# The last tile's store cut into three transfers, and other hand-over semaphores, in a scores kernel

## The chip, the cores and the metric

The kernel runs on one core of one Trainium2 chip. The metric is the device time of one execution in microseconds (us), the median of several runs. The core has a matrix engine (TensorE, PE in the profile), three engines that work on elements (VectorE or DVE, ScalarE or ACT, GpSimd or POOL), an engine that only issues transfers and handles semaphores (SyncE, SP), and 16 DMA engines that move data between the chip's main memory and the on-chip buffers. TensorE's results arrive in a small accumulation memory (PSUM), from which ACT and DVE copy them into the large on-chip memory (SBUF); stores to main memory start from there.

## The reference

```
batch, heads, seq, dim = 8, 8, 512, 64        # q and k: float32
scale = 1.0 / sqrt(dim)
out = einsum('bhqd,bhkd->bhqk', q, k) * scale # float32, 8 x 8 x 512 x 512
```

For each of the 64 pairs of batch and head, the product of q and the transposed k, scaled. The inputs are 16.8 MB, the output is 67.1 MB.

## The kernel before, in words

**Units and tiles.** The inputs are handled in four units of two batches (`UNITS`). A unit's k and q are loaded by one transfer each of 2 MB (`load`, L80). The output is produced in 16 tiles of 4 MB (`CHUNKS * UNITS`). A tile covers four heads of one batch: 128 rows (partitions), each with two runs of 16 KB that are contiguous in main memory (`out_r[g]`, L46). A tile is held in one of three SBUF buffers `bigs`, which serve as load buffers at the start and as store buffers afterwards (`store_buffer`, L77: buffers 0, 2, 1 in turn).

**Preparing the operands.** POOL casts the loaded float32 to bf16 (`cast`, L126, into `xb`, in places straight into `xs`). For each unit there are four chunks that must be transposed. From the second unit on, POOL copies a chunk from `xb` into the staging buffer `xs` (`fill`, L121), PE transposes it into the PSUM tile `tp` (`turn`, L164), and ACT and DVE each move a half of it into the operand buffers `kT` (keys) and `qz` (queries) (`move`, L214). One chunk is handled within each of the first 12 tiles, between its third and fourth pair of matmuls.

**Computing a tile.** PE runs a loop over the 16 tiles (L200). A tile has eight steps p, each with two matmuls that fill one of three PSUM buffers `pss[p % 3]` (`scores`, L182). ACT evicts the even steps and DVE the odd ones, with the scaling, into the store buffer (`evacuator`, L231). The order on every engine is written out by hand, and the engines hand over by semaphores.

**Semaphores.** `next` lets PE begin a tile. `free0a` to `free2b` say that a PSUM buffer has been evicted; six names alternate, as the lists `before` and `after` (L176) have it. PE waits for one of them, and the first matmul behind the wait counts it down again when it completes (L190). `ready` says that a chunk lies in `xs`, `turn` that PE has transposed it, `moved` that ACT and DVE have put it away, `cast` and `room` that load buffers have been read.

**SP.** SP issues everything that moves between main memory and SBUF. For each tile it waits until both evictors have ended their last step (`out`, two counts a tile), issues the store of 4 MB as one transfer, then waits until the store two tiles earlier has landed (`landed`, L98; for the first two tiles, until POOL has read the load buffer, `room`), and only then raises `next`. So a tile starts when the store buffer it writes is free, and SP's issue of the store before it stands in that chain. Each transfer counts a semaphore up by 16 when it has landed.

**POOL at the end.** Behind the casts, POOL copies ten chunks into `xs` (L159 to L161), each as soon as PE has transposed the chunk before it.

Of the kernel before, what the change touches and what calls it, by code (L numbers as in the profile page):

```python
# [5 lines left out]
def kernel(  # L6
# [5 lines left out]
    nc = tc.nc  # L12
    B, H, S, D = q.shape
    scale = 1.0 / (D ** 0.5)
    P = 128
    UNITS = B // 2
# [4 lines left out]
    RO = 8  # L21
# [6 lines left out]
    CHUNKS = 4  # L28
    SLOTS = 12
    PAIRS = RO  # L30
# [4 lines left out]


    names = ["ready", "room", "moved", "zeroed", "ident", "turn", "pe_act", "pe_dve",
             "next", "free0a", "free0b", "free1a", "free1b", "free2a", "free2b",
             "out", "cast"]
    sem = {name: nc.alloc_semaphore(name) for name in names}  # L40
    load_sems = [nc.alloc_semaphore(f"load{n}") for n in range(2 * UNITS)]
    store_sems = [nc.alloc_semaphore(f"store{n}") for n in range(3)]

    q_r = q.rearrange("(v b) g (m j) d -> v (b g m) (j d)", b=2, j=R)
    k_r = k.rearrange("(v b) g (m j) d -> v (b g m) (j d)", b=2, j=R)
    out_r = out.rearrange("(v b) (t x h) (u i) k -> (v b t) (h u) x (i k)", b=2, x=2, h=2, i=RO)  # L46
# [5 lines left out]
    qz = nc.alloc_sbuf_tensor("qz", [P, 2 * N, RO, P], bf16)[:]  # L52
    identity = nc.alloc_sbuf_tensor("identity", [P, P], f32)[:]
    tp = nc.alloc_psum_tensor("tp", [P, W, P], f32)[:]
    pss = [nc.alloc_psum_tensor(f"ps{n}", [P, 2, S], f32)[:] for n in range(3)]

    def words(ap):
        return ap.bitcast(f32)
# [7 lines left out]
    xsw = words(xs.rearrange("p w s d e -> p w (s d e)"))  # L66
    keys = kT.rearrange("p n m s j -> p n (m s j)")

    pe = nc.tensor
# [7 lines left out]
    def store_buffer(g):  # L77
        return bigs[(0, 2, 1)[g % 3]]

    def load(v, x):  # L80
        nc.sync.dma_start(out=xf(v)[:, x],
                          in_=(k_r, q_r)[x][v].rearrange("p (s c) -> p s c", s=2)
                          ).then_inc(load_sems[2 * v + x], 16)
# [6 lines left out]
    tc.compile()  # L90


    nc.sync.wait_ge(sem["room"], 1)
    nc.sync.sem_inc(sem["next"], 1)
    for x in range(2):
        nc.sync.wait_ge(sem["cast"], x + 1)
        load(UNITS - 1, x)
    def landed(g):  # L98
        nc.sync.wait_ge(store_sems[g % 3], 16 * (g // 3 + 1))

    for g in range(CHUNKS * UNITS):
        nc.sync.wait_ge(sem["out"], 2 * g + 2)
        nc.sync.dma_start(out=out_r[g], in_=store_buffer(g).rearrange("p x i k -> p x (i k)")  # L103
                          ).then_inc(store_sems[g % 3], 16)
        if g < CHUNKS * UNITS - 1:
            if g >= 2:
                landed(g - 2)
            else:
                nc.sync.wait_ge(sem["room"], g + 2)
            nc.sync.sem_inc(sem["next"], 1)  # L110
    for n in range(3):
        nc.sync.wait_ge(store_sems[n], 16 * len(range(n, 4 * UNITS, 3)))


    nc.gpsimd.memset(identity, 0.0).then_inc(sem["ident"], 1)
# [2 lines left out]
                            fill=1.0, base=0, pattern=[[-1, P]], channel_multiplier=1  # L118
                            ).then_inc(sem["ident"], 1)

    def fill(copy, c):  # L121
        w0 = c % SLOTS * W
        copy(out=xs.rearrange("p w s d e -> p (w s d e)"),  # L123
             in_=xb[:, w0:w0 + W].rearrange("p w s d e -> p (w s d e)")).then_inc(sem["ready"], 1)

    def cast(v, x, s, j0, j1, dst):  # L126
        src = xf(v)[:, x, s]
        if x == 0:
            src = src.rearrange("p (j e d) -> p j e d", e=2, d=D)[:, j0:j1]
            dst = dst[:, :, s].rearrange("p j d e -> p j e d")  # L130
        else:
            src = src.rearrange("p (j e i d) -> p j e i d", e=2, i=RO, d=D)
            dst = dst[:, :, s].rearrange("p (i j) d e -> p j e i d", i=RO)
        return nc.gpsimd.tensor_copy(out=dst, in_=src)  # L134

    for v in range(UNITS):
        for x in range(2):
# [4 lines left out]
            if v == 1 and x == 0:  # L142
# [3 lines left out]
                last = cast(v, x, 1, 0, W, xs)  # L146
                last.then_inc(sem["ready"], 1)
            else:
                for s in range(2):
                    last = cast(v, x, s, 0, JP, xb[:, w0:w0 + JP])  # L150
# [5 lines left out]
                nc.gpsimd.drain().then_inc(sem["cast"], 1)  # L156
            elif v == 1 and x == 1:
                last.then_inc(sem["cast"], 1)
    for c in range(CHUNKS + 2, CHUNKS * UNITS):  # L159
        nc.gpsimd.wait_ge(sem["turn"], c)  # L160
        fill(nc.gpsimd.tensor_copy, c)  # L161


    def turn(src, dst):  # L164
        for w in range(W):
            ins = pe.transpose(out=dst[:, w], identity=identity, in_=src[:, w])  # L166
            if w == 0 and dst is tp and src is xsw:
                ins.then_inc(sem["ready"], -1)
        ins.then_inc(sem["turn"], 1)

    def take(name, count=1):
        pe.wait_ge(sem[name], count).then_inc(sem[name], -count)  # L172

    before = ["next", None, "free2a", "free0a", "free1a", "free2b", "free0b", "free1b"]  # L176
    after = ["free0a", "free1a", "free2b", "free0b", "free1b", "free2a", "out", "out"]

    def weights(n2, p, w):
        return qz[:, bass.ds(n2 + p // 4, 1), p % 4 * 2 + w].rearrange("p n c -> p (n c)")  # L180

    def scores(n2, p):  # L182
        for w in range(2):
            if w == 0 and before[p]:
                pe.wait_ge(sem[before[p]], 1)
            ins = pe.matmul(out=pss[p % 3][:, w, :], lhsT=weights(n2, p, w),  # L186
                            rhs=keys[:, bass.ds(n2 + p // 4, 1)].rearrange("p n c -> p (n c)"),
                            start=True, stop=True)
            if w == 0 and before[p]:
                ins.then_inc(sem[before[p]], -1)  # L190
        ins.then_inc(sem["pe_dve" if p % 2 else "pe_act"], 1)

    pe.wait_ge(sem["ident"], 2)
# [1 line left out]
    for c in range(CHUNKS):  # L195
        take("ready")
        turn(xw[:, c * W:(c + 1) * W], first[c])
    take("moved", 4 * CHUNKS)
    pe.sem_inc(sem["free2a"], 1)
    with pe.Fori(0, CHUNKS * UNITS) as g:  # L200
        n2 = g % (2 * TILES) * 2
        for p in range(3):
            scores(n2, p)
        with pe.If(g < CHUNKS * (UNITS - 1)):
            pe.wait_ge(sem["ready"], 1)
            turn(xsw, tp)
        for p in range(3, PAIRS):
            scores(n2, p)
        with pe.If(g < CHUNKS * (UNITS - 1)):
            take("moved", CHUNKS)  # L210
# [3 lines left out]
    def move(copy, c, s, tile_):  # L214
        v, t = divmod(c, CHUNKS)
        n0 = v % 2 * N
        h0 = t % 2 * W
        if t < 2:
            src = tile_[half(s)].rearrange("d j (n h m) -> d h n m j", n=N, h=2)
        else:  # L220
            src = tile_[half(s)].rearrange("d (i jj) (n h m) -> d h i n m jj", jj=JJ, n=N, h=2)
            h0 = t % 2 * IW
        for h in range(2):
            if t < 2:
                dst = kw[half(h), n0:n0 + N, :, s, h0:h0 + W]
            else:
                dst = qw[half(h), n0:n0 + N, h0:h0 + IW, h * U // 2:(h + 1) * U // 2].rearrange(
                    "d n i (m s jj) -> d s i n m jj", s=2, jj=JJ)[:, s]
            copy(out=dst, in_=src[:, h]).then_inc(sem["moved"], 1)  # L229

    def evacuator(engine, copy, scaled, parity, done):  # L231
        if parity:
            for v in range(2):
                engine.memset(qz[:, v * N:(v + 1) * N], 0.0).then_inc(sem["zeroed"], 1)  # L234
        for c in range(CHUNKS):
            engine.wait_ge(sem["turn"], c + 1)
            if c == 2:
                engine.wait_ge(sem["zeroed"], 2)
            move(copy, c, parity, first[c])
        count = 0  # L240
        for g in range(CHUNKS * UNITS):
            o = store_buffer(g)
            for p in range(parity, PAIRS, 2):
                x, i = p // 4, p % 4 * 2
                count += 1
                engine.wait_ge(done, count)
                scaled(o[:, x, i:i + 2, :], pss[p % 3]).then_inc(sem[after[p]], 1)
                c = g + CHUNKS
                if p in (1, 2) and c < CHUNKS * UNITS:
                    engine.wait_ge(sem["turn"], c + 1)  # L250
                    move(copy, c, parity, tp)
            if g == 0 and not parity:
                fill(copy, CHUNKS + 1)

    evacuator(nc.scalar, nc.scalar.copy,
              lambda o, ps: nc.scalar.mul(out=o, in_=ps, mul=scale),  # L256
              0, sem["pe_act"])
    evacuator(nc.vector, nc.vector.tensor_copy,
              lambda o, ps: nc.vector.tensor_scalar(out=o, in0=ps, scalar1=scale, scalar2=None,  # L259
                                                    op0=mult),  # L260
              1, sem["pe_dve"])


# [28 lines left out]
```

## Time and profile before

| | |
|---|---|
| Runs | 202.41, 202.66 and 202.81 us; median 202.66 |
| Profiled execution | 202.81 us, of which the span from the first to the last instruction is 201.5 (201.46) us |
| Moved | 16.78 MB read, 67.11 MB written; 416 GB/s over the span |
| Stores | 16, each 4 MB, issued at 32.1 to 180.3 us; 14.9 to 22.2 us from issue to landing, 17.9 in the median |
| Loads | 8, each 2 MB |
| Matmuls of the scores (L186) | 256, mean 469 ns |
| Evictions | DVE 64, mean 1223 ns; ACT 64, mean 1024 ns |
| POOL casts (L134) | 16, mean 2322 ns; copies into `xs` (L123) 10, mean 1896 ns |

How to read it: the profile gives, for each engine, the time in which it executed instructions; a slice view cuts the span, or a window of it, into 40 equal parts and gives the busy share in tenths, for DMA the mean over the 16 DMA engines, with the bytes moved below it. A window view gives the busy time of each engine in a stretch, the granted clock of TensorE, the DMA share and the rate. The chain of waits follows the work that ended last back from step to step. `SPq` is SP's instruction sequence, where issues and semaphore operations lie; L followed by a number is a line of the kernel. "Issue to landing" is the time from a transfer's issue until all engines that carry it have reported.

### The profile page before, as it was taken

Reading aid. Unit: us, or ns where it says so; the run is one execution under the profiler, and the core shown is the slowest. Engines: PE = TensorE matmul, PEld = TensorE weight load, DVE = VectorE, ACT = ScalarE, POOL = GpSimd, SP = SyncE. Lnnn points to the kernel's source line nnn. Section 1 sums busy time; section 2 is a strip of 40 time slices with the busy share of each in tenths; the row PEclk is TensorE's granted clock in tenths of the full one; section 3 lists DMA queues with packets and bytes.
Section 4 is the critical chain, followed back from the end, with each engine's and each line's share of the span. In section 5 each row is a group of like instructions: output and inputs, shape, how many; then the busy total and the mean of one; then the engine's idle time right before and its main releaser. Section 6 shows DMA issues by size and latency. Waiting matters only on the chain.

```text
span 201.5 us, 1491 instructions
## 1 busy us (share of the span) xinstructions
PE 102.4 (51%) x384; PEld 51.4 (25%) x384; DVE 106.1 (53%) x98; ACT 87.4 (43%) x98; POOL 58.4 (29%) x34
## 2 busy tenths in 40 slices
PE   0027481275756575753939394657546575750000
PEld 0026240132424243431506051333112121210000
DVE  0666673074747576768384856957562727260000
ACT  0205665073746464655555464756543434440000
POOL 0399999999303030302121130300000000000000
PEclk9999979588888888799696969978885858575555
DMA  5999999999999999999999999999999999999993
GB/s 185 429 429 439 433 426 423 439 403 436 426 426 446 426 423 431 434 429 420 449 426 423 439 436 423 426 442 429 420 436 436 423 433 436 429 416 426 439 429 137
DMA packets 5506, 83.90 MB, mean 416 GB/s; under 512 B 384, under 2 KB 384, under 8 KB 384
## 3 DMA queue, kind: packets, MB, share of 16 engines
q1 hardware_dynamic: 5504, 83.89, 97.9%
q14 instruction: 2, 0.02, 0.0%
HBM read 16.78 MB, written 67.11 MB: 416 GB/s over the span
## 4 chain that ended last, share of the span: by engine, by line
PE 28%; DVE 21%; DMA 15%; POOL 14%; POOLq 5%; issue 4%; SPq 2%; ACT 1%
PE ps L186 20%; DVE big L259 15%; POOL xb L134 13%; DMA out_dram<-big 11%; PE tp L166 7%; POOLq L154 5%; DVE qz L229 4%; DMA big<-in_k_dram 4%; DVE kT L229 2%; SPq L103 2%; POOL xs L134 1%; POOLq L156 1%; ACT big L256 1%; SPq L110 0%; SPq L90 0%
## 5 line engine op out<-in xcount | busy, mean ns | idle before, releaser
L186 PE MATMUL ps<-kT,qz 128*128 x256 | 81.7, 469 | 61.4 <-SPq L110 42.0
L259 DVE TENSOR_SCALAR big<-ps 128x1024 f32<-128x1024 f32 x64 | 77.0, 1223 | 52.0 <-PE ps L186 50.6
L256 ACT ACTIVATE big<-ps 128x1024 f32<-128x1024 f32 x64 | 65.3, 1024 | 70.2 <-PE ps L186 69.9
L186 PEld LDWEIGHTS ps<-kT,qz 128*128 x256 | 28.4, 111 | 106.9 <-issue 96.9
L134 POOL CAST xb<-big 128x2048 bf16<-128x2048 f32 (+1 forms) x16 | 36.2, 2322 | 3.6 <-DMA big<-in_k_dram 3.1
L123 POOL COPY xs<-xb 128x2048 bf16<-128x2048 bf16 x10 | 19.0, 1896 | 62.0 <-PE tp L166 61.9
L166 PE MATMUL tp<-identity,xs 128*128 128x128 f32 x96 | 19.8, 376 | 0.0
L166 PEld LDWEIGHTS tp<-identity,xs 128*128 128x128 f32 x96 | 18.2, 206 | 4.7 <-issue 4.1
L229 DVE COPY kT<-tp 64x512 f32<-64x512 f32 x14 | 9.7, 694 | 9.1 <-PE tp L166 8.9
L229 ACT COPY kT<-tp 64x512 f32<-64x512 f32 x14 | 8.1, 579 | 13.1 <-PE tp L166 12.9
L229 DVE COPY qz<-tp 64x512 f32<-64x512 f32 x12 | 8.3, 695 | 4.9 <-PE tp L166 4.6
L234 DVE MEMSET qz<- 128x4096 uint32 x2 | 6.9, 3472 | 6.8 <-PEq L90 6.0
L166 PE MATMUL tp<-identity,xb 128*128 128x128 f32 x8 | 1.9, 424 | 13.9 <-PEq L172 13.9
L229 ACT COPY qz<-tp 64x512 f32<-64x512 f32 x12 | 7.5, 622 | 2.1 <-PE tp L166 2.0
L166 PEld LDWEIGHTS tp<-identity,xb 128*128 128x128 f32 x8 | 1.6, 224 | 13.8 <-issue 13.8
L166 PE MATMUL ps<-identity,xb 128*128 128x128 f32 x24 | 3.9, 323 | 1.2 <-PEq L172 1.2
L166 PEld LDWEIGHTS ps<-identity,xb 128*128 128x128 f32 x24 | 3.5, 171 | 1.6 <-issue 1.6
L229 ACT ACT_TABLE_LOAD x1 | 1.3, 1283 | 5.0 <-PEq L90 5.0
L229 DVE COPY qz<-ps 64x512 f32<-64x512 f32 x4 | 2.8, 694 | 1.0 <-PE ps L166 0.9
L229 ACT COPY qz<-ps 64x512 f32<-64x512 f32 x4 | 2.5, 629 | 1.2 <-PE ps L166 1.1
L134 POOL CAST xs<-big 128x1024 bf16<-128x1024 f32 x2 | 2.7, 1337 | 0.2 <-DMA big<-in_k_dram 0.2
L123 ACT COPY xs<-xb 128x2048 bf16<-128x2048 bf16 x1 | 1.9, 1890 | 0.0
(8 smaller groups left out, 3.5 us busy)
## 6 DMA issues: line engine op xcount, KB each, us to landing
out_dram<-big SPq DMA_DIRECT2D x16, 4096.0 KB, 17.9
big<-in_k_dram SPq DMA_DIRECT2D x4, 2048.0 KB, 15.5
big<-in_q_dram SPq DMA_DIRECT2D x4, 2048.0 KB, 17.8
```

The lines of the kernel that those rows point to most:

```text
L103: nc.sync.dma_start(out=out_r[g], in_=store_buffer(g).rearrange("p x i k -> p x (i k)")).then_inc(store_sems[g % 3], 16)
L123: copy(out=xs.rearrange("p w s d e -> p (w s d e)"), in_=xb[:, w0:w0 + W].rearrange("p w s d e -> p (w s d e)")).then_inc(sem["ready"], 1)
L134: return nc.gpsimd.tensor_copy(out=dst, in_=src)
L154: nc.gpsimd.drain().then_inc(sem["room"], 1)
L156: nc.gpsimd.drain().then_inc(sem["cast"], 1)
L166: ins = pe.transpose(out=dst[:, w], identity=identity, in_=src[:, w])
L186: ins = pe.matmul(out=pss[p % 3][:, w, :], lhsT=weights(n2, p, w), rhs=keys[:, bass.ds(n2 + p // 4, 1)].rearrange("p n c -> p (n c)"), sta ...
L229: copy(out=dst, in_=src[:, h]).then_inc(sem["moved"], 1)
L234: engine.memset(qz[:, v * N:(v + 1) * N], 0.0).then_inc(sem["zeroed"], 1)
L256: lambda o, ps: nc.scalar.mul(out=o, in_=ps, mul=scale),
L259: lambda o, ps: nc.vector.tensor_scalar(out=o, in0=ps, scalar1=scale, scalar2=None, op0=mult),
```

## The change

Three things change.

**The last store.** The first 15 tiles are stored as before. The last tile's store is issued as three transfers: the first 12 KB of every 16 KB run, of all 128 rows; the last 4 KB of each run of rows 0 to 119; the last 4 KB of each run of rows 120 to 127. Each has its own semaphore, and SP waits for all three at the end.

**Who raises what.** SP raises `next` as soon as both evictors have finished a tile, before it issues the store, and no longer waits for an earlier store to land. POOL does that waiting: behind each of its copies into `xs` it waits for the store two tiles back and raises `room`. PE takes `next` before the first matmul of a tile and `room` before the second.

**How PE waits.** The six `free` names become three, and `out` becomes one name for each evictor. PE's wait and the count-down are one instruction ahead of the matmul (`take`), where before the matmul carried the count-down.

```diff
-    nc.sync.wait_ge(sem["room"], 1)
-    nc.sync.sem_inc(sem["next"], 1)
     for x in range(2):
         nc.sync.wait_ge(sem["cast"], x + 1)
         load(UNITS - 1, x)
-    def landed(g):
-        nc.sync.wait_ge(store_sems[g % 3], 16 * (g // 3 + 1))
-
+    edge = 3 * RO * S // 4
+    parts = [(slice(0, P), slice(0, edge)), (slice(0, P - 8), slice(edge, RO * S)),
+             (slice(P - 8, P), slice(edge, RO * S))]
+    last = CHUNKS * UNITS - 1
     for g in range(CHUNKS * UNITS):
-        nc.sync.wait_ge(sem["out"], 2 * g + 2)
-        nc.sync.dma_start(out=out_r[g], in_=store_buffer(g).rearrange("p x i k -> p x (i k)")
-                          ).then_inc(store_sems[g % 3], 16)
-        if g < CHUNKS * UNITS - 1:
-            if g >= 2:
-                landed(g - 2)
-            else:
-                nc.sync.wait_ge(sem["room"], g + 2)
-            nc.sync.sem_inc(sem["next"], 1)
+        nc.sync.wait_ge(sem["out_act"], g + 1)
+        nc.sync.wait_ge(sem["out_dve"], g + 1).then_inc(sem["next"], 1)
+        src = store_buffer(g).rearrange("p x i k -> p x (i k)")
+        if g < last:
+            nc.sync.dma_start(out=out_r[g], in_=src).then_inc(store_sems[g % 3], 16)
+        else:
+            for n, (rows, cols) in enumerate(parts):
+                nc.sync.dma_start(out=out_r[g][rows, :, cols], in_=src[rows, :, cols]
+                                  ).then_inc(part_sems[n], 16)
...
-    for c in range(CHUNKS + 2, CHUNKS * UNITS):
-        nc.gpsimd.wait_ge(sem["turn"], c)
-        fill(nc.gpsimd.tensor_copy, c)
+    for g in range(2, CHUNKS * UNITS - 1):
+        if g + CHUNKS < CHUNKS * UNITS:
+            nc.gpsimd.wait_ge(sem["turn"], g + CHUNKS)
+            fill(nc.gpsimd.tensor_copy, g + CHUNKS)
+        nc.gpsimd.wait_ge(store_sems[(g - 2) % 3], 16 * ((g - 2) // 3 + 1)
+                          ).then_inc(sem["room"], 1)
...
     def scores(n2, p):
+        x, i = p // 4, p % 4 * 2
+        if p != 1:
+            take(f"free{p % 3}" if p else "next")
+        ps = pss[p % 3]
         for w in range(2):
-            if w == 0 and before[p]:
-                pe.wait_ge(sem[before[p]], 1)
-            ins = pe.matmul(out=pss[p % 3][:, w, :], lhsT=weights(n2, p, w),
-                            rhs=keys[:, bass.ds(n2 + p // 4, 1)].rearrange("p n c -> p (n c)"),
+            if p == 0 and w == 1:
+                take("room")
+            ins = pe.matmul(out=ps[:, w, :],
+                            lhsT=qz[:, bass.ds(n2 + x, 1), i + w].rearrange("p n c -> p (n c)"),
+                            rhs=keys[:, bass.ds(n2 + x, 1)].rearrange("p n c -> p (n c)"),
                             start=True, stop=True)
-            if w == 0 and before[p]:
-                ins.then_inc(sem[before[p]], -1)
         ins.then_inc(sem["pe_dve" if p % 2 else "pe_act"], 1)
...
-                scaled(o[:, x, i:i + 2, :], pss[p % 3]).then_inc(sem[after[p]], 1)
+                scaled(o[:, x, i:i + 2, :], pss[p % 3]).then_inc(
+                    sem[f"free{p % 3}"] if p < PAIRS - 2 else drained, 1)
```

`take(name)` is a wait for one count and its decrement in one instruction of PE; it was there before for `moved` and for the first four transposes. `drained` is `out_act` for ACT and `out_dve` for DVE.

More of the change, by code (lines that the diff above doesn't have):

```diff
@@ L37 @@
     names = ["ready", "room", "moved", "zeroed", "ident", "turn", "pe_act", "pe_dve",
-             "next", "free0a", "free0b", "free1a", "free1b", "free2a", "free2b",
-             "out", "cast"]
+             "next", "free0", "free1", "free2", "out_act", "out_dve", "cast"]
     sem = {name: nc.alloc_semaphore(name) for name in names}
@@ L42 @@
     store_sems = [nc.alloc_semaphore(f"store{n}") for n in range(3)]
+    part_sems = [nc.alloc_semaphore(f"part{n}") for n in range(3)]
     q_r = q.rearrange("(v b) g (m j) d -> v (b g m) (j d)", b=2, j=R)
@@ L97 @@
         load(UNITS - 1, x)
-    def landed(g):
-        nc.sync.wait_ge(store_sems[g % 3], 16 * (g // 3 + 1))
+    edge = 3 * RO * S // 4
+    parts = [(slice(0, P), slice(0, edge)), (slice(0, P - 8), slice(edge, RO * S)),
+             (slice(P - 8, P), slice(edge, RO * S))]
+    last = CHUNKS * UNITS - 1
     for g in range(CHUNKS * UNITS):
-        nc.sync.wait_ge(sem["out"], 2 * g + 2)
-        nc.sync.dma_start(out=out_r[g], in_=store_buffer(g).rearrange("p x i k -> p x (i k)")
-                          ).then_inc(store_sems[g % 3], 16)
-        if g < CHUNKS * UNITS - 1:
-            if g >= 2:
-                landed(g - 2)
-            else:
-                nc.sync.wait_ge(sem["room"], g + 2)
-            nc.sync.sem_inc(sem["next"], 1)
+        nc.sync.wait_ge(sem["out_act"], g + 1)
[7 more added lines that the diff above has]
+                                  ).then_inc(part_sems[n], 16)
     for n in range(3):
-        nc.sync.wait_ge(store_sems[n], 16 * len(range(n, 4 * UNITS, 3)))
+        nc.sync.wait_ge(store_sems[n], 16 * len(range(n, last, 3)))
+    for n in range(3):
+        nc.sync.wait_ge(part_sems[n], 16)
     nc.gpsimd.memset(identity, 0.0).then_inc(sem["ident"], 1)
@@ L166, in turn @@
             ins = pe.transpose(out=dst[:, w], identity=identity, in_=src[:, w])
-            if w == 0 and dst is tp and src is xsw:
-                ins.then_inc(sem["ready"], -1)
         ins.then_inc(sem["turn"], 1)
@@ L172, in take @@
         pe.wait_ge(sem[name], count).then_inc(sem[name], -count)
[L176 to L180, printed above, removed]
     def scores(n2, p):
+        x, i = p // 4, p % 4 * 2
+        if p != 1:
+            take(f"free{p % 3}" if p else "next")
+        ps = pss[p % 3]
         for w in range(2):
-            if w == 0 and before[p]:
-                pe.wait_ge(sem[before[p]], 1)
-            ins = pe.matmul(out=pss[p % 3][:, w, :], lhsT=weights(n2, p, w),
-                            rhs=keys[:, bass.ds(n2 + p // 4, 1)].rearrange("p n c -> p (n c)"),
+            if p == 0 and w == 1:
[3 more added lines that the diff above has]
+                            rhs=keys[:, bass.ds(n2 + x, 1)].rearrange("p n c -> p (n c)"),
                             start=True, stop=True)
-            if w == 0 and before[p]:
-                ins.then_inc(sem[before[p]], -1)
         ins.then_inc(sem["pe_dve" if p % 2 else "pe_act"], 1)
@@ L198 @@
     take("moved", 4 * CHUNKS)
-    pe.sem_inc(sem["free2a"], 1)
+    for name in ("next", "free2"):
+        pe.sem_inc(sem[name], 1)
     with pe.Fori(0, CHUNKS * UNITS) as g:
@@ L204 @@
         with pe.If(g < CHUNKS * (UNITS - 1)):
-            pe.wait_ge(sem["ready"], 1)
+            take("ready")
             turn(xsw, tp)
@@ L229, in move, with evacuator @@
             copy(out=dst, in_=src[:, h]).then_inc(sem["moved"], 1)
-    def evacuator(engine, copy, scaled, parity, done):
+    def evacuator(engine, copy, scaled, parity, done, drained):
         if parity:
@@ L256 @@
               lambda o, ps: nc.scalar.mul(out=o, in_=ps, mul=scale),
-              0, sem["pe_act"])
+              0, sem["pe_act"], sem["out_act"])
     evacuator(nc.vector, nc.vector.tensor_copy,
@@ L260 @@
                                                     op0=mult),
-              1, sem["pe_dve"])
+              1, sem["pe_dve"], sem["out_dve"])
 _INS = ['q', 'k']
```

## The prediction

> **What bounds the kernel now.** I read the page's slices first, because they tell whether any compute engine can set the end.
>
> ```profile
> PE 102.4 (51%) x384; PEld 51.4 (25%) x384; DVE 106.1 (53%) x98; ACT 87.4 (43%) x98; POOL 58.4 (29%) x34
> DMA  5999999999999999999999999999999999999993
> GB/s 185 429 429 439 433 426 423 439 403 436 426 426 446 426 423 431 434 429 420 449 426 423 439 436 423 426 442 429 420 436 436 423 433 436 429 416 426 439 429 137
> q1 hardware_dynamic: 5504, 83.89, 97.9%
> ```
>
> The reader is to see that no compute engine passes 53%, while the 16 DMA engines are full in all but the first and the last slice, at about 430 GB/s. 83.9 MB have to pass, and nothing in the middle can be gained without moving fewer bytes. What is left is the edges. The last slice carries 137 GB/s, so I opened the end, in 40 slices of 0.11 us.
>
> ```profile
> DMA  9369999090000300000300003000003000000000
> GB/s 583 146 291 583 437 583 437 0 437 0 0 0 0 146 0 0 0 0 0 146 0 0 0 0 146 0 0 0 0 0 146 0 0 0 0 0 0 0 0 0
> q1 hardware_dynamic: 44, 0.46, 24.1%
> ```
>
> The window is 197.0 to 201.5 us. A packet counts in the slice in which it starts, and one of 16 KB makes 146 GB/s there. Up to 198.0 several engines start packets. After that there are exactly four starts, at 198.5, 199.2, 199.8 and 200.4: one engine alone, four packets behind the other 15. Its last packet starts at 200.39 and ends at 201.0; the landing, 0.46 us later, ends the span. The last packets of the others start by 197.94, so they are through by 198.55. 15 engines stand idle for 2.45 us.
>
> The rate of one engine comes from a stretch without compute, at 434 GB/s, and one with it, at 431:
>
> ```profile
> 182.00:192.00 10.00, 0.00 (x0) 0.00 (x0) 0.00 (x0) 0.00 (x0) 0.00 (x0) 0.50 1.02 434
> 61.70:71.40 9.70, 6.12 (x27) 3.40 (x26) 6.19 (x6) 5.43 (x7) 1.90 (x1) 0.85 1.01 431
> ```
>
> By share, 431/1.01/16 = 26.7 GB/s for an engine, so 16 KB take 0.61 us and 64 KB 2.45 us. That the queue is never empty is seen from the stores' landing times.
>
> ```profile
> DMA to landing us min/median/max: 14.9/17.9/22.2
> ```
>
> A store puts 256 KB on each engine, 9.8 us, and lands 0.46 us later, 10.3 in all. The quickest of the 16 took 14.9, so even it waited 4.6 us behind the store before it. That wait is the cover for everything that happens ahead of a store's issue. It counts for the slowest engine; the quickest of the 16 were about 1 us further at that store (the landing records of the store before it span 0.96 us), which leaves some 3.7 us. By the last store it is 21.2 us to landing, some 8 us of cover on the quick engines.
>
> The chain around a hand-over of tiles is the last view.
>
> ```profile
> 57.84 0.02 issue
> 57.85 0.37 SPq L103
> 58.23 0.05 issue
> 58.27 0.02 SPq L110
> 58.29 0.30 issue
> 58.59 2.50 PE ps L186 x6
> ```
>
> From the last eviction of a tile to the next tile's first matmul 0.75 us pass, half of it SP's issue of the store.
>
> **The change, part by part.** The sum is made against the profiled execution, 202.81 us with a span of 201.46 (1.35 lie around it). The median of the runs is 202.66, 0.15 below, and the forecast is put on it.
>
> *The last store's cut.* Now each engine gets 8 rows x 2 x 16 KB = 256 KB. Afterwards the first part gives each of 16 engines 8 x 2 x 12 KB = 192 KB; the 120 rows over 15 engines give 8 x 2 x 4 KB = 64 KB each; the 8 rows over 8 engines give 8 KB each. So one engine carries 192 KB, eight carry 264 and seven 256. If the relieved one is the straggler, its end goes from 201.00 to 201.00 - 2.45 = 198.55, just where the others end now. An engine with 264 KB ends 8 KB/26.7 GB/s = 0.31 us later. Two engines share the last place at 198.54 to 198.55 and 8 of those 15 get the extra rows, so 1 - (7/15 x 6/14) = 0.8 that one of the two does: I take 0.31 whole, with 0 as the lower bound.
>
> *Smaller packets.* 16 or 18 packets of 4 KB are added per engine, 12 KB instead of 16 in the rest, and two more completion packets (0.009 us each in the packet records). The trace has no data packet of 4 KB. The nearest row is the instruction queue's two packets of 8 KB near 80.4 us, at 0.309 us each: twice that is 0.618, against 0.611 for one of 16 KB, so 0.007 for a cut. 16 cuts make 0.11. Bounds: 0 (time goes by bytes), and ten times the row, 0.07 a cut, 1.1 us in all. I take 0.11, since 8 KB is the nearest size.
>
> *Three issues for one.* SP issues in 0.37 us, so the third part leaves 0.75 us later, at about 181.4. The engines reach the last store only when store 14 is through, after 188. Hidden by some 7 us of queue; without that it would cost 0.75. The final waits on three semaphores in place of one are 0.017 us each, and only the last to be filled counts: 0.03.
>
> *Hand-over.* SP now raises `next` before it issues the store, so the first matmul of a tile may start 0.37 us earlier; `room` moves to POOL, is taken before the second matmul, and no longer sits between SP's store and `next`. PE's waits carry their own decrement in place of a matmul's; their number is alike, plus 16 for `room`, at 0.017 us for such an instruction in SP's rows (0.3 in all). All this lies ahead of a store's issue: cover 3.7 us at the worst store, so it yields 0 and costs 0. Without cover it would gain 0.37 a tile, about 4 us over the first eleven tiles that compute paces.
>
> *POOL's new waits.* Behind each wait for store g-2 stands the copy for chunk g+5 (1.90 us, L123), on which PE's transposes of tile g+1 wait, and behind them the moves on ACT and DVE. Up to tile 8 the landing comes 3 us or more before the tile starts. It is tightest at tile 11: store 8 lands near 132.6, the copy would end at 134.5, and PE transposed there at 135.2. Room of 0.7 us; if it is gone, the tile slips by the lateness and its store, issued some 7 us before its turn, still comes in time. 0, with bounds of 0 and, were the queue empty, 1.9 for each of ten copies.
>
> Sum: the end of the packets moves from 201.00 to 198.55 + 0.31 + 0.11 = 198.97, 2.03 earlier, less 0.03 for the waits: 202.81 - 2.0 = 200.8 for a profile, **200.65** for the median.
>
> *Is the straggler the relieved one?* No view numbers the engines. The packet records allow this: within 4 ns each packet starts where the one before it on its engine ends, which ties them into 16 chains. The straggler shows from about 43 us on: of its 16 packets in 10 us, 10 to 15 last longer than 0.611 us, of the others almost none until 150. Where it begins, at 43, its chain leads back to the engine that was the last of 16 to start in the first load (3.12 us; the first at 1.97). If shares are given out in the order of the numbers, as those starts suggest, that is the highest number, and 120 rows over 15 engines leave out that one. The lag grows only while tiles are computed and stands still in the last two stores, so it will be there afterwards. Chains can be swapped where two engines are in step; I give this 0.85.
>
> [...]
>
> **Rivals.**
>
> A. *The straggler is one of the eight that get more.* Then its end moves out: 0.31 for 8 KB and 0.11 for the cuts give 202.66 + 0.42 = 203.1, slower. For it: half of the engines are in that set, and a chain may have been swapped. Against: the trace-back to the last starter. [...]
>
> B. *It is one of the other seven, or the 120 rows go over all 16.* Its bytes stay (or fall by 4 KB, 0.15): 202.66 + 0.11, about 202.7, no change.
>
> C. *The lag is not the same.* The straggler's delay grows with the tiles at 0.2 to 0.25 us each; were it half as large again, its end would stay 1.2 us behind: 201.6. The same time results if a cut costs ten times its row: 200.65 + 1.0 = 201.6.
>
> D. *The queue runs dry* through POOL's new place in the hand-over. It needs more than 3.7 us of delay piled up by tile 5; each copy that comes late costs up to 1.9, so the first two only eat the cover and the third and fourth would show whole: 200.65 + 3.8 = 204.4.
>
> **How the numbers follow.** Forecast 0.78 with its own range 200.1 to 201.2 (0.31 spared on one side, 0.5 for cuts and lag on the other); C 0.07; A 0.07; B 0.06; D 0.02. A measurement of this kernel can tell about 0.2%, 0.4 us, from no change. Faster: 0.78 + 0.07 = 0.85. A lies at that border, so I leave it 0.05 of slower and 0.02 of same; with D's 0.01 each: slower 0.06, same 0.09. The range 200.0 to 201.7 takes in the forecast and C and leaves out the rest.
>
> **What would show it.** The end opened as above: no lone packets, all engines done within some 0.5 us. The span near 199.4 to 199.5. Three issues on SP at about 180 and no slice in the middle below 400 GB/s; hand-over chains without SP's issue in them. Wrong: four lone packets again (B), or more than four packets' time (A); a hole between two stores (D).

## The result, and the profile after

The changed kernel takes 203.34 us in the median (203.22 to 203.65, 4 runs), the kernel before 202.62 (202.41 to 202.81): a ratio of 1.0038, 95% interval 1.0021 to 1.0056. It is slower by about 0.7 us, where 200.65 was forecast. The profiled execution took 203.34 us with a span of 202.00.

The page of the changed kernel: busy time, slices, the transfers' queue.

```profile
PE 104.4 (52%) x384; PEld 50.6 (25%) x384; DVE 106.3 (53%) x98; ACT 87.2 (43%) x98; POOL 58.5 (29%) x34
...
DMA  6999999999999999999999999999999999999995
GB/s 198 428 435 432 425 438 422 428 393 438 425 428 441 425 425 441 422 425 451 422 422 448 422 425 441 425 428 425 444 428 422 444 425 422 441 423 428 419 378 163
DMA packets 5786, 83.91 MB, mean 415 GB/s; under 512 B 407, under 2 KB 407, under 8 KB 663
...
q1 hardware_dynamic: 5783, 83.89, 98.4%
```

As before, no engine is busy for more than 53% and the DMA slices are full in all but the first and the last. 256 packets of 4 KB are new (663 less 407). The last two slices hold the difference: the last but one carries 378 GB/s, where it was 429. The end opened again in 40 slices, now from 197.0 to 202.0:

```profile
DMA  9999585795997958877665333231100100000000
GB/s 229 197 262 197 131 164 164 229 360 197 459 328 295 361 164 328 328 262 295 197 229 197 131 164 131 98 131 66 66 33 33 66 33 33 0 33 0 0 0 0
DMA packets 220, 0.82 MB, mean 165 GB/s; under 512 B 25, under 2 KB 25, under 8 KB 217
```

Before, 15 engines ended together at 198.55 and one ran on alone. Here the engines are busy and move half as much (some 200 GB/s, where it was 426 from 182 to 195), and they end one after the other until 201.5. Two things are to be told apart in it: who ends last, and why the others end so late.

The middle is as it was. The issue rows of the changed kernel's stores and of the last three transfers:

```profile
L107 SPq DMA_DIRECT2D out_dram<-big x15: 372/372/402, 34.7 to 169.7; - x15
...
DMA to landing us min/median/max: 14.8/18.4/22.3
```
```profile
180.08 3.15 SPq L110 DMA_DIRECT2D out_dram<-big  x3
```

The shortest time from issue to landing is 14.8 us (14.9 before), against the 10.3 that a store takes by itself (the prediction's estimate), so the queue never ran dry. The three issues took 3.15 us together, not 3 x 0.37: 0.37 for the first, 1.40 and 1.28 for the two behind it. That is far ahead of the queue's turn, so it is hidden, as forecast.

The landing records tell who ended last. For each transfer of the changed kernel, in us of the span, the last landing and the one before it (an issue over k engines leaves k of them and one entry at the issue for the rest):

```
store 14, 16 engines      191.90  (189.58)
12 KB x 128 rows, 16      199.19  (198.42)
4 KB x 120 rows, 15       201.66  (201.05)
4 KB x 8 rows, 8          201.96  (201.37)
```

From 191.90 to 199.19 lie 7.29 us, 16 packets of 12 KB at 0.456. To 201.66 it is another 2.47, 16 packets of 4 KB at 0.155 with nobody in the way, and to 201.96 another 0.30, two more. That is one engine working without a pause, the straggler (the engine that ends alone), and it has a share in the 15-engine part and in the 8-engine part. Before, from store 14's last landing to the end it was 9.69 us; now it is 10.06. The straggler was not relieved but given 8 KB more: rival A.

### The profile page after: what moved, and what is told of

It is laid out like the page before. It is cut to its first block, busy times and chain, and to the rows that moved or that the text cites. A ratio compares the mean times of both kernels' runs of the same rounds, so it can differ in the third digit from the quotient of the medians.

```text
span 202.0 us, 1636 instructions
## 1 busy us (share of the span) xinstructions
PE 104.4 (52%) x384; PEld 50.6 (25%) x384; DVE 106.3 (53%) x98; ACT 87.2 (43%) x98; POOL 58.5 (29%) x34
## 5 line engine op out<-in xcount | busy, mean ns | idle before, releaser
L187 PE MATMUL ps<-kT,qz 128*128 x256 | 83.8, 464 | 58.8 <-PEq L176 58.6
L187 PEld LDWEIGHTS ps<-kT,qz 128*128 x256 | 27.9, 109 | 106.8 <-issue 99.8
L172 PEld LDWEIGHTS tp<-identity,xs 128*128 128x128 f32 x96 | 16.5, 190 | 5.6 <-issue 5.1
L172 PE MATMUL tp<-identity,xs 128*128 128x128 f32 x96 | 17.6, 344 | 0.5 <-PEq L176 0.5
L172 PE MATMUL ps<-identity,xb 128*128 128x128 f32 x24 | 5.6, 422 | 1.2 <-PEq L176 1.2
L172 PEld LDWEIGHTS ps<-identity,xb 128*128 128x128 f32 x24 | 5.0, 228 | 1.6 <-issue 1.6
```

What stands on the lines that cost most here:

```text
L187: ins = pe.matmul(out=ps[:, w, :], lhsT=qz[:, bass.ds(n2 + x, 1), i + w].rearrange("p n c -> p (n c)"), rhs=keys[:, bass.ds(n2 + x, 1)].re ...
```

## The experiments

Each run stands beside runs of the kernel before on the same chip; "before" is 202.45 to 202.55 in these.

### The two halves of the change apart

The hand-over alone, the changed kernel with one last store:

```diff
-        if g < last:
-            nc.sync.dma_start(out=out_r[g], in_=src).then_inc(store_sems[g % 3], 16)
-        else:
-            for n, (rows, cols) in enumerate(parts): ...
+        nc.sync.dma_start(out=out_r[g], in_=src).then_inc(store_sems[g % 3], 16)
```

> The changed kernel with the last store in one transfer again: the hand-over alone. Theory H0 (the hand-over lies in the cover of the store queue): 202.6, within 0.3 of before; one engine four packets behind the others at the end, as before. Rival H1 (the hand-over makes the straggler's lag or the queue worse): 202.9 to 203.3, and then the cut itself is nearly neutral.

Measured: 202.82, ratio 1.0019 (1.0009 to 1.0028). Slower by 0.35 us, which lies between the two expectations; the interval does not reach a ratio of 1. It comes back below.

The cut alone, the kernel before with the three transfers:

```diff
-        nc.sync.dma_start(out=out_r[g], in_=store_buffer(g)...).then_inc(store_sems[g % 3], 16)
+        for n, (rows, cols) in enumerate(parts):      # 128 x 12 KB, 120 x 4 KB, 8 x 4 KB
+            nc.sync.dma_start(out=out_r[g][rows, :, cols], in_=src[rows, :, cols]
+                              ).then_inc(part_sems[n], 16)
```

> The kernel before, with only the last store changed to the three transfers of the changed kernel. Theory C (the cut alone makes the loss): 203.2, with the end of the trace as in the changed kernel: three engines or fewer active after 200.5, the last one 0.3 us after the straggler's 15-engine part. Rival H1 (the hand-over makes it): 202.6 to 202.8.

Measured: 203.14, ratio 1.0031 (1.0018 to 1.0044), and the same end: the straggler lands its parts at 199.21, 201.70 and 202.01, again 2.49 and 0.31 apart. Theory C holds; the cut makes the larger part of the loss. Measured apart, cut and hand-over cost 0.67 and 0.35 us, 1.0 together, where the whole change costs 0.72. The intervals (0.4 to 0.9, 0.2 to 0.6 and 0.4 to 1.1) allow for this, so how the two share the loss is known only roughly.

### Packets of 4 KB, without narrow transfers

```diff
+    parts = [(slice(0, P), slice(0, edge)), (slice(0, P), slice(edge, RO * S))]   # 12 KB, 4 KB
```

> The kernel before, with the last store cut in two by columns only: 12 KB and 4 KB of every run, both over all 128 rows and so over 16 engines. Theory N (what stretches the 4 KB packets in the changed kernel is the split over 15 engines): the 256 packets of 4 KB take 0.16 us each here, the 15 engines end within 0.2 us of where they ended before (198.55), the straggler by 201.2; 202.8. Rival M (4 KB pieces at a pitch of 16 KB are slow in themselves): a mean of 0.21 us or more, the engines end as late as 200 to 201; 203 or more.

Measured: 202.54, ratio 1.0007 (0.9998 to 1.0016). The 256 packets of 4 KB take 0.163 us in the mean; in the changed kernel it is 0.213, in the run of the cut alone 0.224. Window views of the end, this run and then the run of the cut alone (start and end, length, five engines, clock, DMA share, GB/s):

```profile
196.50:197.50 1.00, 0.00 (x0) 0.00 (x0) 0.00 (x0) 0.00 (x0) 0.00 (x0) 0.50 1.01 406
197.50:198.50 1.00, 0.00 (x0) 0.00 (x0) 0.00 (x0) 0.00 (x0) 0.00 (x0) 0.50 0.83 332
198.50:199.50 1.00, 0.00 (x0) 0.00 (x0) 0.00 (x0) 0.00 (x0) 0.00 (x0) 0.50 0.07 29
```
```profile
196.50:197.50 1.00, 0.00 (x0) 0.00 (x0) 0.00 (x0) 0.00 (x0) 0.00 (x0) 0.50 0.99 225
197.50:198.50 1.00, 0.00 (x0) 0.00 (x0) 0.00 (x0) 0.00 (x0) 0.00 (x0) 0.50 0.85 242
198.50:199.50 1.00, 0.00 (x0) 0.00 (x0) 0.00 (x0) 0.00 (x0) 0.00 (x0) 0.50 0.83 283
```

At the same busy share, 0.99 against 1.01, the cut over 15 engines moves 225 GB/s and the one over 16 moves 406. So packets of 4 KB were cheap over 16 engines: 0.163 us, where a quarter of the 0.611 for 16 KB is 0.153. Over 15 the packets lasted longer for the same bytes. Theory N holds: what stretches the packets is the split over 15 engines, not their size.

### Which engine is the straggler

No record numbers the engines. Here and below a number, and "lowest", stands for the place in the order in which wider and wider transfers take the engines in, on the assumption that these sets are nested. The last 1.5 KB of each run taken off all and given to seven engines:

```diff
+    tail = slice(RO * S - 384, RO * S)
+    parts = [(slice(0, P), slice(0, RO * S - 384)), (slice(0, 119), tail),
+             (slice(119, 126), tail), (slice(126, P), tail)]
```

> The kernel before, with the last store's last 1.5 KB of each run taken off all 16 engines (24 KB each) and given to the lowest seven: 119 rows and 7 rows over 7 engines, the last two rows over two. Each of the seven nets 30 KB more. Theory S7 (the straggler has number 7, or any number above 6): it ends 24 KB / 26.7 GB/s = 0.9 us earlier, at 200.1, the seven at 198.55 + 1.2 + 0.15 = 199.9 if they do not hinder one another: 201.8. If they do, up to twice the time for their 54 KB, they end near 201.7 and nothing is won: 203. Theory S0 (it is one of the lowest seven): it ends 1.1 us later, 203.9. With theory S15 (number 15) as with S7; the changed kernel's own end tells these two apart.

Measured: 203.88, ratio 1.0074 (1.0060 to 1.0088). This is S0's time, but engines that hinder one another could give it too, so the packet records decide: the straggler ends its share of the 16-engine part at 199.69, and from 199.70 to 201.78 follow 34 packets of 1.5 KB back to back at 0.061 us, which is the share of one of the seven (17 rows x 2), then two more. The straggler is one of the seven. It ends there, without a share in the two-row transfer; another engine, which has one, ends 0.03 us later.

One run with transfers of different widths gives the number:

```diff
+    parts = [(slice(0, P), slice(0, edge)), (slice(0, 112), tail), (slice(112, 118), tail),
+             (slice(118, 123), tail), (slice(123, 127), tail), (slice(127, P), tail)]
```

> The kernel before, with the last 1.5 KB of each run stored by transfers over 16, 6, 5, 4 and 2 engines (112, 6, 5, 4 rows, and the two runs of row 127), so that the number of these transfers in which the straggler lands last tells its number. From the run with seven engines it is none of 7 to 15, and since it has no part of the two-row transfer there, it is one of 2 to 6. Number 6: it is last only in the transfer over 16, the others have landed by 199.5. Number 5: last also in the one over 6; number 4: also over 5; number 3 or 2: also over 4. Each share adds 0.12 us to the end. A rival, that no engine is the straggler for good and the lag wanders: last in none of them by more than 0.5 us.

Measured: 203.12, one run. The last landing of each transfer, and the one before it:

```
16 engines, first part    200.39  (198.84)
16 engines                201.21  (199.80)
 6 engines                201.41  (199.98)
 5 engines                201.60  (200.17)
 4 engines                200.35  (200.32)
 2 engines                200.10  (199.95)
```

In four of them one engine lands 1.4 to 1.6 us behind the next; it has a part in the transfer over five and none in the one over four. If transfers over k engines use nested sets, which every run here fits, it has number 4, counted from 0 in the order in which the sets take engines in. The change relieved number 15.

### Relieving the right one

The last 768 bytes of each run to the four below it:

```diff
+    edge = RO * S - 192
+    parts = [(slice(0, P), slice(0, edge)), (slice(0, 124), tail), (slice(124, P), tail)]
```

> The kernel before, with the last 768 bytes of each run taken off all 16 engines (12 KB each) and given to the lowest four by transfers of 124 and 4 rows. The tagged run says that the straggler has number 4, just outside the four. Theory F (it is number 4): it ends 12 KB / 26.7 GB/s = 0.45 us earlier; the four get 64 packets of 768 bytes at some 0.033 us, 2.1, and end at 198.9 - 0.45 + 2.1 = 200.5, just ahead of it, if they do not hinder one another: 202.05, the first version faster than before. Rival (it is one of the four): it carries the 2.1 us itself, 204.1. If the four contend as the seven did, they end 1 us or more later and the time is 202.5 or above.

Measured: 203.80, ratio 1.0064 (1.0050 to 1.0078). The straggler lands at 200.60 and has no part in the rest, as theory F has it: relieved as computed. But the four land between 201.4 and 202.2 with their 124 rows and by 202.35 with the rest; their packets take 0.049 us in the mean, where an unhindered one takes 0.036.

The same four, with half as many packets, twice as long (the last 1.5 KB of the second run of each row only), and rows chosen apart: rows 0 to 91 in one transfer (23 each), then nine transfers of rows nine apart. That the four would hinder one another less in this way was the author's guess:

```diff
+    parts = [(slice(0, P), 0, slice(0, RO * S)), (slice(0, P), 1, slice(0, edge)),
+             (slice(0, 92), 1, tail)] + [(slice(92 + c, P, 9), 1, tail) for c in range(9)]
```

> [...] The straggler loses 12 KB as before, 0.45 us, and lands at 200.6; each of the four gets 32 packets of 1.5 KB at 0.061 us, 1.96. [...] Rival Q (few engines contend anyhow, or main memory is what they contend for): packets of 0.1 us and more in the middle, the four land after 201; 202.5 to 203.5.

Measured: 203.85, ratio 1.0068 (1.0054 to 1.0081). The four's packets take 0.085 us in the mean instead of 0.065. The long ones, 0.2 to 0.45, lie between 197.7 and 200.0, while other engines still had packets of their own; after that all take 0.065. The last packet ends at 201.12. The landings come later still: each engine's landings of the nine small transfers are 0.17 to 0.19 us apart, where its packets are 0.067 apart, and the last comes at 202.50, 1.39 us behind the last packet; in the kernel before that distance is 0.43. So the time is rival Q's, but about 0.95 us of it lies between the packets and their landings, which the expectation did not have. Without it the end would be near 201.55 (an estimate), still later than the 201.0 to 201.4 of the kernel before. There was no version that beat it.

### What the narrow transfers contend for

Tails over 15 and 14 engines with rows nine apart, and over 15 engines with neighbouring rows:

```diff
+    parts = [(slice(0, P), slice(0, edge))] + [(slice(c, P, 9), tail) for c in range(9)]
```

> The kernel before, with the last 4 KB of each run stored over 15 and 14 engines as in the changed kernel, but by transfers that take every ninth row (rows c, c+9, ...: two of 15 rows, seven of 14). [...] Rival Q (a transfer over fewer than 16 engines contends whatever its rows): a median of 0.2 us or more, engines other than the straggler end after 200.

```diff
+    parts = [(slice(0, P), slice(0, edge))] + [(slice(r, min(r + 15, P)), tail) for r in range(0, P, 15)]
```

> The kernel before, with the last 4 KB of each run stored over 15 engines by eight transfers of 15 neighbouring rows, and one of 8 rows: the counterpart of the run with rows nine apart. [...]

Measured: 203.18, ratio 1.0030 (1.0020 to 1.0040), for rows nine apart, packets of 4 KB at 0.176 us in the mean, the others through by 199.9; 204.52, ratio 1.0100 (1.0071 to 1.0130), for neighbouring rows, packets at 0.298, the longest 2.55. The window of 196.5 to 197.5 of the two:

```profile
196.50:197.50 1.00, 0.00 (x0) 0.00 (x0) 0.00 (x0) 0.00 (x0) 0.00 (x0) 0.50 0.90 324
```
```profile
196.50:197.50 1.00, 0.00 (x0) 0.00 (x0) 0.00 (x0) 0.00 (x0) 0.00 (x0) 0.50 0.60 98
```

Same bytes, nearly the same widths, 324 against 98 GB/s: which rows a transfer takes matters. Rival Q of the run with rows nine apart does not hold: its mean is under 0.2 us, and the others are through before 200. The packets of 4 KB took 0.163 us in the mean in the 16-way split, 0.176 with rows nine apart, 0.213 to 0.224 with 120 neighbouring rows in one transfer, eight to an engine, and 0.298 with 15 neighbouring rows in one, one to an engine. Rows nine apart do not rule contention out: the longest packet there took 0.433, and in the run with rows chosen apart, where other engines read beside the four, their packets took 0.085 us in the mean instead of 0.065. The rows also fix the addresses in main memory, which no run here varies by themselves. What the engines contend for is not shown.

### Where the lag comes from

600 semaphore instructions more on SP, then on POOL, and 128 on PE, each on a semaphore nobody waits for and in time that the engine had to spare:

```diff
             nc.sync.sem_inc(sem["next"], 1)
+            for n in range(40):
+                nc.sync.sem_inc(sem["spare"], (1, -1)[n % 2])
```

> The kernel before, with 40 semaphore instructions added on SP after each release of a tile, 600 in all, on a semaphore that nobody waits for. SP has 5 us and more to spare in each tile, so nothing waits for them. Theory I (the straggler is the engine that also carries something for each instruction executed, which would explain why the lag grows only while tiles are computed, and why the hand-over alone, with 145 more recorded instructions, is 0.35 us slower): the lag grows from 2.5 to 2.5 x 2091/1491 = 3.5 us, 203.5. Rival W (the lag has to do with the data traffic of the engines): 202.5, lag unchanged.

> The kernel before, with 60 semaphore instructions on POOL behind each of its ten copies into xs, 600 in all, where POOL idles. Theory I2 (the straggler pays for instructions of any engine): its lag grows by some 4.7 us as with SP's 600, 207. Rival V (it pays for SP's alone, whose sequence shares something with the transfers): lag 2.5, 202.5.

> The kernel before, with 8 semaphore instructions on PE at the end of each tile, 128 in all, about as many as the changed hand-over has more than before in its profile (126). Theory I2 with the price of 7.8 ns from SP's 600: the lag grows by 1.0 us, 203.5; at the mean price of the kernel's own instructions, 2.5 us / 1491 = 1.7 ns, by 0.2, 202.7. If it comes out at 202.8 like the hand-over alone, the number of instructions is enough to account for that; if at 202.5, the hand-over's loss has another cause.

Measured: 207.38, ratio 1.0234 (1.0209 to 1.0259) for SP; 204.66, ratio 1.0107 (1.0091 to 1.0122) for POOL; 202.87, ratio 1.0018 (1.0009 to 1.0027) for PE. The end of the run with 600 on SP, in 40 slices from 196.0 to 206.2:

```profile
DMA  9779799301010010101001010010101001010000
GB/s 450 321 321 643 321 514 450 129 0 64 0 64 0 0 64 0 64 0 64 0 0 64 0 64 0 0 64 0 64 0 64 0 0 64 0 64 0 0 0 0
```

15 engines end where they did before, just after 198; the lone one now follows with twelve packets instead of four. Over the profiled executions (lag: last landing of store 14 less the median of its 16 landings):

| Profiled execution | lag, us | time, us | time less lag |
|---|---|---|---|
| cut over 16 engines | 2.51 | 202.46 | 199.95 |
| hand-over alone | 2.88 | 202.68 | 199.80 |
| before | 2.97 | 202.81 | 199.84 |
| 128 more on PE | 3.10 | 202.84 | 199.74 |
| 600 more on POOL | 4.68 | 204.52 | 199.84 |
| 600 more on SP | 7.70 | 207.50 | 199.80 |

The time is the lag plus 199.8: the median of the engines keeps its schedule, and the straggler sets the end. The profiled execution before lies above its kernel's medians beside these runs (202.81 against 202.45 to 202.55), so the rows do not show a larger lag for the hand-over; its 0.35 us rests on the medians of 11 and 22 runs. An added instruction costs the straggler 4.92 us / 600 = 8 ns on SP, 3.7 on POOL and 3.1 on PE. Theory I falls in its price for SP (1.7 ns) and stands in its kind. The straggler pays for these instructions, whichever engine runs them; by what path stays open. All that were added are semaphore operations, so whether other instructions cost the same was not tried. Each of these executions was recorded by the profiler, so that the recording itself is the traffic is not excluded.

## Why the prediction was wrong

**What held.** The bound (the 16 DMA engines), the reading of the end (one engine, four packets behind), the price of a cut by itself, the cover of the queue: none of the rivals of a dry queue came true, and the copies on POOL held nothing up. With SP's issue out of the chain, PE began a tile 0.51 us after the last eviction instead of 0.75, and as forecast that was worth nothing. The third issue was out at 183.2 instead of the forecast's 181.4, still hidden.

**The step that failed: "Is the straggler the relieved one?", 0.85.** It is number 4, not 15. The prediction tied packets into chains by 4 ns and followed the straggler back to the engine that started last. Two engines in step can be swapped in such a chain, which the text said, and that the starts come in the order of the numbers was an assumption that no row bore. Rival A, priced at 203.1 and given 0.07, is what happened: 0.30 us measured for the two packets more (0.31 forecast), 0.07 for cuts and completions (0.11), and 0.15 because the straggler landed store 14 that much later in this execution (191.90 against 191.75). That is 0.52 of the 0.54 from the span's 201.46 to 202.00. The medians differ by 0.72, since the profiled execution before lies 0.19 above its median. No view numbered the engines, and on the rows' own evidence the relieved one was one of 16; the chance should have been near that, and the forecast with it.

**A second step would have spoilt it: "16 cuts make 0.11".** The cut was cheap where the transfer was split over 16 engines (202.54, ratio 1.0007). Over 15 and 8 the other engines' last landing was at 201.37 instead of 198.90. Had number 15 been the straggler, the end would by this record have been near 201.4 all the same, against 201.46 before: an estimate, by which there was nothing to win. The upper bound of ten times the row, 1.1 us, was too narrow; the nearest row was two packets of the instruction queue, and the price lies in the packets of the narrow transfers: 0.213 us in the mean for 4 KB, against 0.163 over 16 engines.

**A third: the hand-over "yields 0 and costs 0".** It costs 0.35 us (1.0019). The cover was right and the account was not. It took the number of PE's instructions to be alike, with 16 more for `room`; the profile has 129 semaphore instructions more on PE and 13 more on POOL. And it counted them on their engines' time alone. 128 on PE that do nothing cost 0.40, so the number is enough to explain the 0.35; that no other cause adds or takes away is not shown.

**How many engines carry a transfer.** No run shown by then had a transfer of fewer than 128 rows, so nothing bore the sum's 15 engines for 120 rows and 8 for 8. The landing records of the changed kernel show these numbers, 15 landings and 8; in the other runs 119 rows gave 7 and 124 gave 4. Which engines they are no record shows, since none numbers them; the straggler's shares fit nested sets.

## What to carry to other kernels

When a kernel is bound by transfers and one DMA engine ends alone, find out which one it is before cutting a transfer for it: a last store in transfers of different widths showed it here in one run, by those in which one engine landed late. A transfer not split over all 16 engines was not the same work on fewer of them: the window of 196.5 to 197.5 had 205 GB/s in the changed kernel, 324 with rows nine apart and 98 with 15 neighbouring rows, where the cut over 16 engines had 406. And in such a kernel semaphore instructions that delay no engine may still cost time, if the lag of the DMA engine that ends last grows with their number (here by 3.1 to 8 ns each).

## What the runs showed that was not expected

- Added instructions slowed a DMA engine: 600 semaphore instructions on idle SP made the kernel 4.92 us longer, with 15 DMA engines on their old schedule. The last store was issued at 184.7 instead of 180.3, still ahead of its turn on these 15. In the kernel before, the lag grows by 0.16 to 0.28 us a store from store 1 to store 9, by 0.09 to 0.17 from there to store 13, and no more in the last two.
- The 600 on POOL made a second engine late, 1.8 us behind the median at the last store; those on SP did not (0.4).
- Of the transfers of a cut last store, the first kept SP for 0.34 to 0.37 us and each one behind it for 1.05 to 1.42, whatever its width: 1.31 for the second one over 16 engines in the run cut by columns. One took 10.06, the third of the run that relieves number 4 by transfers over four engines. Why is not shown.
